# Weight tiles in another order, and a new plan of mixer steps, in a two-layer trunk on one core

## The chip, the core and the metric

The kernel runs on one core of a Trainium2 chip. A core has a matrix engine (PE in the profile; its weight loads are PEld), a vector engine (DVE), a scalar engine (ACT), a general engine (POOL) and a queue that issues transfers (SP). Each works through its own list of instructions in order, and they meet through semaphores. The metric is the device time of one launch in microseconds, the median of several runs. Less is better.

## What is computed

Two layers act on 256 tokens of width 1024, all in 32-bit floats. Cut to what matters:

```
a = rms_norm(h) ; proj = a @ w_in
da_q, da_k, da_v, z, xbc, dt, gla_q, gla_k, gla_v, gla_g, gla_lr = split(proj)
y_da  = differential attention: 4 heads, two softmaxes each, after a norm and a partial rotation of q and k
y_ssd = state-space mixer: conv of 4 taps and silu on xbc, two chunks of 128 tokens, gated by silu(z), norm
y_gla = linear attention: 4 chunks of 64, decays from gla_lr through log-sigmoid, norm, times silu(gla_g)
h = h + concat(y_da, y_ssd, y_gla) @ w_out
h = h + (silu(f @ w_gate) * (f @ w_up)) @ w_down          with f = rms_norm(h)
h = h + sigmoid(h @ ple_gate) * (p @ ple_proj)
```

## The kernel before, in words

All weights, some 133 MB, stream from memory once, in tiles of about 1 MB. Each tile is one unit of the list `units`. A unit's tile lands in a staging buffer `st` (three of them). ACT rounds it to a high part `wh` (L214) and DVE subtracts to get the low part `wl` (L215), both in halves of 1024 columns, with six halves of each kind in the pool. PE then makes three passes per block: high by high, high by low, low by high. The code loads two units ahead of the one that multiplies.

A layer has 19 units for the input products, 6 for the output product, 22 + 16 for the feed-forward part and 4 for the last gate. The change touches the first 25. Of the 19:

- `q0 q1 k0 k1 v0 v1 gv0 gv1 sg0 sg1` are halves of tiles with 512 columns (L884 to L886, 48 passes of 512 columns for a pair of halves). q, k, v belong to the attention, gv and sg are the value and the gate of the linear attention. A pair is read out of the accumulators at the end of its second half: q and k by four squares on ACT (L387) and four sums and products on DVE (L388, L389), v, gv and sg by two ACT instructions (L912).
- `x0` to `x3` (the four convolution tiles) and `gq`, `gk` have 256 columns (L263 to L265, 48 passes of 256 columns). A convolution tile leaves on DVE one product (L573) and six multiply-adds (L582), then a silu on ACT (L584).
- `z0`, `z1` (the state-space gate, the time steps `dt` and the input of the decays) and `ple` (the projection of p, L242 to L244).

Between the passes of a unit stand steps of the four mixers. They are Python generators: `gates` (3 steps), `ssd` (8), `gla` (5) and `da` (13). `PLAN` lists the units in their order, each with the steps that go into it, and `PLAN_OUT` does so for the output product. `spread` puts a unit's steps in a list, and at each `tick` (after 3 passes of an x-tile, 6 of the other kinds) one piece of a step is issued; `'-'` lets a tick go by:

```
        if pending:
            S, name = pending[0]
            with tc.issue_after(last.ins):
                done = name == '-' or step(S, name)
            if done:
                pending.pop(0)
```

Within this, the framework's scheduler decides at build time the order on each engine.

The steps that the prediction speaks of: the decays run L733, L740 (PE), L742 to L744 (ACT: absolute value, exponential, logarithm), L746 (DVE), L752 (PE), L755 and L756 (ACT exponentials). An attention block runs scores L484 and mask L491 (PE), maxima L499 and L500 (DVE), exponentials L504 (ACT, each with a sum that is read out), then L507, L508, L511, L512 (DVE), transposes L469 (PE), products with v L536, L540, L541 (PE). There are three blocks: one for the first 128 tokens and four heads, two for the second 128 tokens and two heads each. The linear attention ends with L817 and L826 (PE), the squares L395 (ACT), the norm L397, L184 to L194, L402 and the product with sg L837 (DVE), the transposes L845 (PE), and the two parts of `mix` L409 (ACT) and L410 (DVE), which the output product reads (L256, L258). PSUM has four banks for the accumulators `acc` and four for everything of the mixers, `pm`, which are used in turn: a mixer's matmul waits until the bank's last tile but three has been read.

Of the kernel before, what the change touches and what calls it, by code (L numbers as in the profile page):

```python
# [76 lines left out]
    ('x0', ()),  # L77
    ('x1', ()),
    ('x2', ()),
    ('z1', ()),  # L80
    ('gq', ()),
    ('x3', ('gates',)),
    ('k0', ('gates', 'ssd')),
    ('k1', ('-', '-', '-', '-', 'gates', 'ssd')),
    ('gk', ('da', 'da', 'ssd')),
    ('gv0', ('ssd',)),
    ('gv1', ('gla', '-', '-', 'da', 'da')),
    ('sg0', ('gla', 'ssd', 'gla')),
    ('sg1', ('-', 'da', 'ssd')),
    ('v0', ('ssd', '-', 'da', '-', 'da')),  # L90
    ('v1', ('ssd', 'da', '-', 'gla')),
    ('ple', ('da', '-', '-', 'da', '-', 'gla')),
]
PLAN_OUT = [('-', '-', 'da'), ('-', '-', 'da'), ('-', '-', 'da'), (), (), ()]


def _two_pi_parts():
# [11 lines left out]
def trunk_kernel(ctx: ExitStack, tc: tile.TileContext, a: dict):  # L109
# [752 lines left out]
    def spread(S, names, go, w):  # L862
        pending.extend((S, n) for n in names)
        go(w)
        while pending:
            tick(turn[0])
# [124 lines left out]
    def out_units(i, S, x):  # L991

        def first(c2):
            def go(w):
                for pb, c, _ in gemm_t(lambda c: (w, c * P), S["mix"][1] + S["mix"][2], True,
                                       0 if c2 else 4):
                    hv = h[:, 2 * c2 + c]
                    dve.tensor_tensor(hv, pb[:, :T], hv, ALU.add)
                    dve.tensor_tensor(hv, pb[:, T:], hv, ALU.add)
            return go  # L1000
# [13 lines left out]
        for c2 in range(4):  # L1014
            units.append((a["w_o1"][i, c2], KD, T,
                          lambda w, go=first(c2), c2=c2: spread(S, PLAN_OUT[c2], go, w)))
        for c4 in range(2):
# [228 lines left out]
```

## Time and profile before

| | |
|---|---|
| runs | 800.24, 800.93, 802.68 us; median 800.93 |
| the profiled execution | 800.33 us, span 798.1 us |
| PE busy | 778.2 us, 98% of the span |
| DVE, ACT busy | 640.9 us (80%), 477.4 us (60%) |
| granted clock of PE | 0.999 of full speed |

The busy share is a mean over the whole span. The 19 input units of the first layer end about 155 us after the span's start, and those of the second begin about 402 us and end about 548 us after it. The mixers' steps lie in these stretches.

### The profile page before, as it was taken

The page shows a single profiled execution, that of the slowest core. Times are in us where ns is not written, and L with a number is a line of the kernel's source. Part 1 is how long each engine was busy: PE and PEld are TensorE (multiplying, and loading weights), DVE is VectorE, ACT ScalarE, POOL GpSimd, SP SyncE. Part 2 cuts the span into 40 slices and gives each one's busy share as a digit, 9 for nine tenths or more (in the row PEclk, how much of TensorE's full clock was granted, in tenths as well). Part 3 has the DMA queues.
Part 4 walks back from the last instruction along what each step waited for, and adds up shares of the span by engine and source line. Part 5 has one row for each costly group of instructions (what it writes and reads, how often), then busy time and mean ns, then how long its engine had stood idle before and what let it go on. Part 6 is the DMA issues. An engine that isn't in the chain of part 4 may idle for free.

```text
span 798.1 us, 12793 instructions
## 1 busy us (share of the span) xinstructions
PE 778.2 (98%) x4810; PEld 682.7 (86%) x4810; DVE 640.9 (80%) x1341; ACT 477.4 (60%) x838; POOL 23.1 (3%) x36
## 2 busy tenths in 40 slices
PE   9999999899999999999999999997999999999997
PEld 6998877789888888888889988786998888888887
DVE  5998998888787777667799779988897777767674
ACT  7778537656665555555667585285466555554553
POOL 2000000002000000000020000000020000000000
PEclk9999999999999999999999999999999999999999
DMA  8763524244655543557555523433455555445641
GB/s 292 284 218 111 172 84 153 82 159 159 211 197 178 206 154 135 184 185 248 208 168 202 172 96 127 159 106 106 168 179 185 207 173 196 159 148 183 198 158 54
DMA packets 24302, 134.92 MB, mean 169 GB/s; under 512 B 2992, under 2 KB 5296, under 8 KB 11696
## 3 DMA queue, kind: packets, MB, share of 16 engines
q1 hardware_dynamic: 23904, 133.57, 48.8%
q8 instruction: 38, 0.62, 0.3%
q0 software_dynamic: 192, 0.52, 0.2%
q14 instruction: 24, 0.20, 0.1%
q10 hardware_dynamic: 144, 0.01, 0.0%
HBM read 133.05 MB, written 1.05 MB: 168 GB/s over the span
## 4 chain that ended last, share of the span: by engine, by line
PE 80%; DVE 14%; DMA 2%; ACT 2%; issue 1%; SPq 0%; DVEq 0%; ACTq 0%
PE acc L256 37%; PE acc L258 18%; DVE wl L215 4%; PE acc L265 4%; PE acc L264 4%; PE acc L263 4%; PE acc L884 2%; PE acc L886 2%; PE acc L885 2%; ACT e L504 1%; DMA h<-in_x 1%; PE acc L243 1%; PE acc L242 1%; PE acc L244 1%; DMA st<-in_w_z 1%
## 5 line engine op out<-in xcount | busy, mean ns | idle before, releaser
L214 ACT ACTIVATE wh<-st 128x1024 fp32r<-128x1024 f32 (+5 forms) x274 | 266.9, 979 | 231.0 <-PE acc L256 101.3
L215 DVE TENSOR_TENSOR wl<-st,wh 128x1024 fp32r<-128x1024 f32 (+5 forms) x274 | 308.5, 1128 | 100.3 <-ACT wh L214 99.8
L256 PE MATMUL acc<-x,wh 128*128 128x512 f32 x800 | 252.2, 396 | 0.1
L258 PEld LDWEIGHTS acc<-x,wl 128*128 128x128 f32 x800 | 150.3, 188 | 35.2
L258 PE MATMUL acc<-x,wl 128*128 128x256 f32 x800 | 157.2, 278 | 0.0
L256 PEld LDWEIGHTS acc<-x,wh 128*128 128x128 f32 x800 | 122.2, 189 | 1.4 <-DVE x L296 0.7
L256 PE MATMUL acc<-act,wh 128*128 128x512 f32 x352 | 111.9, 395 | 0.0
L258 PEld LDWEIGHTS acc<-act,wl 128*128 128x128 f32 x352 | 66.2, 188 | 14.3
L258 PE MATMUL acc<-act,wl 128*128 128x256 f32 x352 | 72.0, 279 | 0.0
L884 PE MATMUL acc<-wh,x 128*128 128x512 f32 x160 | 66.8, 420 | 0.5 <-DVE gate L301 0.4
L265 PE MATMUL acc<-x,wl 128*128 128x256 f32 x224 | 63.4, 283 | 0.9 <-DVE wl L215 0.9
L263 PE MATMUL acc<-x,wh 128*128 128x256 f32 x224 | 63.8, 285 | 0.0
L886 PE MATMUL acc<-wh,x 128*128 128x512 f32 x160 | 63.6, 397 | 0.0
L885 PE MATMUL acc<-wl,x 128*128 128x512 f32 x160 | 63.3, 396 | 0.2 <-DVE wl L215 0.2
L264 PE MATMUL acc<-x,wh 128*128 128x256 f32 x224 | 63.4, 283 | 0.0
L256 PEld LDWEIGHTS acc<-act,wh 128*128 128x128 f32 x352 | 54.9, 189 | 1.3
L265 PEld LDWEIGHTS acc<-x,wl 128*128 128x128 f32 x224 | 42.9, 192 | 1.1 <-DVE wl L215 1.1
L264 PEld LDWEIGHTS acc<-x,wh 128*128 128x128 f32 x224 | 42.9, 192 | 0.3
L263 PEld LDWEIGHTS acc<-x,wh 128*128 128x128 f32 x224 | 42.9, 191 | 0.3
L256 PE MATMUL acc<-mix,wh 128*128 128x512 f32 x128 | 40.8, 401 | 2.3 <-DVE mix L410 2.3
L301 DVE TENSOR_TENSOR gu<-acc,gu 128x256 f32<-128x256 f32 x88 | 36.8, 418 | 2.9 <-ACT gu L300 2.9
L884 PEld LDWEIGHTS acc<-wh,x 128*128 128x128 f32 x160 | 30.3, 190 | 6.9 <-ACT wh L214 0.7
(276 smaller groups left out, 1166.7 us busy)
## 6 DMA issues: line engine op xcount, KB each, us to landing
st<-in_w_f SPq DMA_DIRECT2D x44, 1024.0 KB, 4.9
st<-in_w_d SPq DMA_DIRECT2D x32, 704.0 KB, 4.1
st<-in_w_x SPq DMA_DIRECT2D x18, 1024.0 KB, 4.8
st<-in_w_o SPq DMA_DIRECT2D x12, 1024.0 KB, 5.0
st<-in_w_t SPq DMA_DIRECT2D x11, 1024.0 KB, 4.9
st<-in_w_g SPq DMA_DIRECT2D x8, 1024.0 KB, 4.9
st<-in_w_z SPq DMA_DIRECT2D x3, 1088.0 KB, 5.0
st<-in_w_x SPq DMA_DIRECT2D x8, 256.0 KB, 5.0
```

The lines of the kernel that those rows point to most:

```text
L214: i_hi = act.activation(wh[:, s], st[:, o], AF.Copy)
L215: i_lo = dve.tensor_tensor(wl[:, s], st[:, o], wh[:, s].bitcast(F32), ALU.subtract)
L242: pe.matmul(out, sh, mh, start=i == 0, stop=False)
L256: pe.matmul(out, wh[:, lo:lo + P], x[k], start=k == 0, stop=False)
L258: last = pe.matmul(out[:, :T], wl[:, lo:lo + P], x[k][:, :T], start=False, stop=k == n - 1)
L263: pe.matmul(out, sh, hi, start=k == 0, stop=False)
L264: pe.matmul(out, sh, x[k][:, T:], start=False, stop=False)
L265: last = pe.matmul(out[:, :T], sl, hi, start=False, stop=k == n - 1)
L301: dve.tensor_tensor(out, pb[:, :T], out, ALU.add)
L884: pe.matmul(pb[b], xh, wh, start=kk_ == 0, stop=False)
L885: pe.matmul(pb[b], xh, wl, start=False, stop=False)
L886: last = pe.matmul(pb[b], xl, wh, start=False, stop=kk_ == KD - 1)
```

## The change

The order of the units becomes: q0 q1 z0 x0 x1 x2 **x3 z1 sg0 sg1 k0 k1 gq gk** gv0 gv1 v0 v1 ple. Before it was: q0 q1 z0 x0 x1 x2 z1 gq x3 k0 k1 gk gv0 gv1 sg0 sg1 v0 v1 ple. So the last convolution tile comes ahead of z1, the gate sg comes from behind gv to a place ahead of k, and gq from ahead of x3 to behind k. The mixer steps are dealt anew over these units: the state-space steps stand in k0, k1, gq, gk, gv0, gv1, v0, v1 (before: k0, k1, gk, gv0, sg0, sg1, v0, v1), and one attention step less stands ahead of ple. The output product's plan differs in one entry. No instruction of the mixers or products is added or removed, and the tables hold for both layers.

```
     ('x2', ()),
+    ('x3', ()),
     ('z1', ()),
-    ('gq', ()),
-    ('x3', ('gates',)),
+    ('sg0', ()),
+    ('sg1', ('gates',)),
     ('k0', ('gates', 'ssd')),
...
-    ('v1', ('ssd', 'da', '-', 'gla')),
-    ('ple', ('da', '-', '-', 'da', '-', 'gla')),
+    ('v1', ('ssd', 'da', 'gla')),
+    ('ple', ('da', '-', '-', 'da', '-', 'gla', 'da')),
 ]
...
-PLAN_OUT = [('-', '-', 'da'), ('-', '-', 'da'), ('-', '-', 'da'), (), (), ()]
+PLAN_OUT = [('-', '-', 'da'), ('-', '-', '-', '-', 'da'), ('-', '-', 'da'), (), (), ()]
```

On ACT, in the first layer, this is where the decays (`ge`) are made, before:

```order
L742 ACTIVATE ge_885<-pm_882 128x512
L671 ACT_TABLE_LOAD
L671 ACTIVATE ce_897<-pm_894 128x16
L743 ACTIVATE ge_885<-ge_885 128x512
L214 ACTIVATE wh_1014<-st_1013 128x1024
L584 ACT_TABLE_LOAD
L584 ACTIVATE conv_857<-conv_857 128x512
L744 ACT_TABLE_LOAD
L744 ACTIVATE ge_885<-ge_885 128x512
```

and now:

```order
L742 ACTIVATE ge_898<-pm_895 128x512
L671 ACT_TABLE_LOAD
L671 ACTIVATE ce_910<-pm_907 128x16
L743 ACTIVATE ge_898<-ge_898 128x512
L214 ACTIVATE wh_1027<-st_1026 128x1024
L744 ACT_TABLE_LOAD
L744 ACTIVATE ge_898<-ge_898 128x512
```

The silu of the last convolution tile, with the table load for it, no longer stands between the exponential and the logarithm. The silu of sg moves ahead of L742. In all ACT has 17 table loads in its list instead of 23.

On DVE, the end of the third attention block and the start of the linear attention's norm (`fss`), before. sm_1586 and e_1590 belong to the second block, sm_1638 and e_1642 to the third, wl_1912 to a weight tile of the output product:

```order
L507 RECIPROCAL sm_1586<-sm_1586 128x2x2
L508 TENSOR_SCALAR sm_1586<-sm_1586,lam 128x2
L511 TENSOR_SCALAR e_1593<-e_1593,sm_1586 128x256 x2
L512 SCALAR_TENSOR_TENSOR e_1590<-e_1590,sm_1586,e_1593 128x256 x2
L507 RECIPROCAL sm_1638<-sm_1638 128x2x2
L508 TENSOR_SCALAR sm_1638<-sm_1638,lam 128x2
L410 SCALAR_TENSOR_TENSOR mix_1548<-pm_1667,par_70,mix_1548 128x128
L511 TENSOR_SCALAR e_1645<-e_1645,sm_1638 128x256 x2
L512 SCALAR_TENSOR_TENSOR e_1642<-e_1642,sm_1638,e_1645 128x256 x2
L215 TENSOR_TENSOR wl_1912<-st_1905,wh_1911 128x1024
L410 SCALAR_TENSOR_TENSOR mix_1549<-pm_1667,par_70,mix_1549 128x128
L397 TENSOR_REDUCE fss_1729<-fsq_1727 128x4
```

and now, with the third block's names sm_1673 and e_1677:

```order
L499 TENSOR_REDUCE mx_1672<-pm_1644 128x2
L410 SCALAR_TENSOR_TENSOR mix_1574<-pm_1627,par_70,mix_1574 128x128
L500 TENSOR_SCALAR mx_1672<-mx_1672 128x2x2
L410 SCALAR_TENSOR_TENSOR mix_1575<-pm_1627,par_70,mix_1575 128x128
L507 RECIPROCAL sm_1673<-sm_1673 128x2x2
L508 TENSOR_SCALAR sm_1673<-sm_1673,lam 128x2
L511 TENSOR_SCALAR e_1680<-e_1680,sm_1673 128x256 x2
L512 SCALAR_TENSOR_TENSOR e_1677<-e_1677,sm_1673,e_1680 128x256 x2
L397 TENSOR_REDUCE fss_1725<-fsq_1723 128x4
```

The second block has gone ahead, and between the third block's maxima (L500) and the use of its exponentials' sums (L507) only one short L410 is left.

On PE, from the second transposes of the linear attention's result (L845) on, before. acc_1868 is the last output of the ple projection, mix_1548 to mix_1551 the state-space result, acc_1915 an output of the output product:

```order
L845 MATMUL pm_1894<-cst,fyn_1755 128x128 x4
L256 MATMUL acc_1915<-mix_1548,wh_1781 128x512
L256 MATMUL acc_1915<-mix_1549,wh_1781 128x512
L258 MATMUL acc_1915<-mix_1548,wl_1782 128x256
L258 MATMUL acc_1915<-mix_1549,wl_1782 128x256
```

and now, with acc_1855 as the last output of ple:

```order
L845 MATMUL pm_1862<-cst,fyn_1751 128x128 x4
L242 MATMUL acc_1855<-ph_1038,wh_1615 128x256
L243 MATMUL acc_1855<-pl_1039,wh_1615 128x256
L244 MATMUL acc_1855<-ph_1038,wl_1616 128x256
L242 MATMUL acc_1855<-ph_1038,wh_1620 128x256
L243 MATMUL acc_1855<-pl_1039,wh_1620 128x256
L244 MATMUL acc_1855<-ph_1038,wl_1621 128x256
L536 MATMUL pm_1877<-v_1769,at_1670 128x128 x4
L256 MATMUL acc_1915<-mix_1572,wh_1774 128x512
L256 MATMUL acc_1915<-mix_1573,wh_1774 128x512
```

Six passes of ple and the attention's first products with v (L536) stood ahead of the transposes and stand behind them now.

## Rows read from the trace of the kernel before

**Rows 1.** The page: busy time, share of the span and instructions by engine.

```profile
PE 778.2 (98%) x4810; PEld 682.7 (86%) x4810; DVE 640.9 (80%) x1341; ACT 477.4 (60%) x838; POOL 23.1 (3%) x36
```

**Rows 2.** Waits of PE, whole span: waiter, releaser, total us, times, longest.

```profile
PE pm L845 <- DVE fyn L837: 4.1, 2, 2.0
PE pm L536 <- ACT v L912: 2.5, 2, 1.2
PE acc L256 <- DVE mix L410: 2.3, 2, 1.2
...
PE pm L484 <- DVE gst L804: 1.2, 2, 0.7
PE pm L484 <- ACT e L504: 1.1, 2, 0.6
```

**Rows 3.** DVE by windows, one in each layer: length, busy, clock, DMA, GB/s.

```profile
79.00:154.90 75.90, 70.73 (x198) 1.00 0.38 129
471.30:547.30 76.00, 70.74 (x198) 1.00 0.37 129
```

**Rows 4.** Longest wait of DVE between 79 and 155 us: total, times, longest.

```profile
DVE sm L507 <- ACT e L504: 2.5, 3, 1.7
```

**Rows 5.** Timeline of PE: start, length; passes of 512, of 256 columns, k's end.

```profile
134.64 0.39 PE L885 MATMUL acc<-wl,x 128*128 128x512 f32 x1
134.87 0.39 PE L886 MATMUL acc<-wh,x 128*128 128x512 f32 x1
...
182.90 0.28 PE L263 MATMUL acc<-mix,wh 128*128 128x256 f32 x1
183.02 0.28 PE L264 MATMUL acc<-mix,wh 128*128 128x256 f32 x1
...
77.02 0.28 PE L263 MATMUL acc<-x,wh 128*128 128x256 f32 x1
```

**Rows 6.** Timeline of DVE: the decays, k's eviction, a weight split, the last gate product.

```profile
72.95 0.69 DVE L746 SCALAR_TENSOR_TENSOR gk<-pm,ge 128x512 f32<-128x512 f32 x1 [2.67 <-ACT ge L744]
...
78.96 0.41 DVE L388 TENSOR_REDUCE dss<-dsq 128x4 f32<-128x256 f32 x1
...
81.58 1.22 DVE L215 TENSOR_TENSOR wl<-st,wh 128x1024 fp32r<-128x1024 f32 x1
82.72 0.37 DVE L426 TENSOR_SCALAR dv<-dss,rr 128x16 f32<-128x16 f32 x2
...
154.16 0.76 DVE L837 TENSOR_TENSOR fyn<-fyn,sg 128x256 f32<-128x256 f32 x2
```

**Rows 7.** Timeline of ACT around the decays.

```profile
69.05 1.28 ACT L584 ACT_TABLE_LOAD   x1
70.34 0.63 ACT L584 ACTIVATE conv<-conv 128x512 f32<-128x512 f32 x1
```

**Rows 8.** Timeline of DVE and of ACT: exponentials of the first and the third block.

```profile
123.97 0.17 DVE L500 TENSOR_SCALAR mx<-mx 128x8 f32<-128x8 f32 x1
127.18 0.20 DVE L507 RECIPROCAL sm<-sm 128x8 f32<-128x8 f32 x1 [1.73 <-ACT e L504]
...
140.51 0.47 ACT L504 ACTIVATE e<-pm,mx 128x256 f32<-128x256 f32 x1
142.21 0.22 ACT L504 ACTIVATION_READ_ACCUMULATOR e<-pm,mx 128x1 f32 x1
```

**Rows 9.** Timeline of PE from the linear attention's last products to the output product.

```profile
144.02 1.09 PE L826 MATMUL pm<-gst,gq 64*64 64x128 f32 x24
...
148.24 0.71 PE L536 MATMUL pm<-v,at 128*128 128x128 f32 x4 [1.22 <-ACT v L912]
...
154.73 0.79 PE L845 MATMUL pm<-cst,fyn 128*128 128x128 f32 x4 [2.03 <-DVE fyn L837]
155.27 0.72 PE L256 MATMUL acc<-mix,wh 128*128 128x512 f32 x2
...
161.26 1.20 PE L256 MATMUL acc<-mix,wh 128*128 128x512 f32 x4 [1.15 <-DVE mix L410]
```

More of the change, by code (lines that the diff above doesn't have):

```diff
@@ L79 @@
     ('x2', ()),
+    ('x3', ()),
     ('z1', ()),
-    ('gq', ()),
-    ('x3', ('gates',)),
+    ('sg0', ()),
+    ('sg1', ('gates',)),
     ('k0', ('gates', 'ssd')),
[L84 to L90, printed above, removed]
-    ('v1', ('ssd', 'da', '-', 'gla')),
-    ('ple', ('da', '-', '-', 'da', '-', 'gla')),
+    ('k1', ('-', '-', 'gates', 'ssd')),
+    ('gq', ('ssd', 'da', 'da')),
+    ('gk', ('ssd', '-', 'da')),
+    ('gv0', ('da', 'ssd')),
+    ('gv1', ('gla', 'ssd', '-', 'da')),
+    ('v0', ('gla', '-', 'da', 'ssd', 'gla')),
+    ('v1', ('ssd', 'da', 'gla')),
+    ('ple', ('da', '-', '-', 'da', '-', 'gla', 'da')),
 ]
-PLAN_OUT = [('-', '-', 'da'), ('-', '-', 'da'), ('-', '-', 'da'), (), (), ()]
+PLAN_OUT = [('-', '-', 'da'), ('-', '-', '-', '-', 'da'), ('-', '-', 'da'), (), (), ()]
 def _two_pi_parts():
```

## The prediction

> **What bounds the kernel now.** I read the page first. PE is busy for 778.2 of 798.1 us [rows 1], so 20 us is all that any reordering can return, and the start and the end of the program take part of it. The list of PE's waits says where the rest lies [rows 2]. The five largest belong to the input units and the step into the output product; together they make 11.2 us, half in each layer. Four are waits for DVE or ACT behind a mixer's step: the transposes of the linear attention's result wait for the gate product (L845, 4.1), the attention's first products for v (L536, 2.5), the output product for `mix` (L256, 2.3), the scores for a bank of PSUM (L484).
>
> The windows say why. From the eviction of k to the last gate product (L837), DVE works 70.73 of 75.90 us in the first layer and 70.74 of 76.00 in the second [rows 3]. In this stretch DVE is the bound and PE, with 3.2 us of waits at L536 and L845, follows it. The reader is to see in [rows 3] that the two layers behave alike, so I work out one and double it. The DVE idles 5.2 us in the stretch; 2.5 of that are three waits for the exponentials of an attention block [rows 4], the rest are smaller waits and the gaps between short dependent instructions.
>
> So the question for the new order is not how PE's work is laid, which stays the same, but when DVE enters this stretch, how much work lies in it, how long it idles there, and what PE still has to do when it ends.
>
> **The change part by part.** The sum is made against the profiled execution, 800.33 us with a span of 798.1; the median of the runs shown stands 0.6 above it.
>
> *Entry into the stretch.* Ahead of k's end PE gains the pair sg and loses gq. A pass of 512 columns follows its predecessor after 0.23 us, one of 256 columns after 0.12 [rows 5]; 48 passes each make 10.9 and 5.75, so k's products end 5.15 us later. Before, PE was through with k at 77.02 [rows 5] but DVE came to it at 78.96 [rows 6], 1.94 late. It was late because it had stood 2.67 us for the logarithm of the decays [rows 6], and the logarithm stood on ACT behind a table load and the silu of x3 [rows 7]. With x3 ahead this pair is gone from there. DVE then enters when the first square of k's eviction is read, some 0.4 after PE (an estimate from the 0.41 of L388's row, of the same size [rows 6]). Entry: +5.15 - 1.94 + 0.4 = +3.6. If the logarithm comes late all the same, +5.15; less than +3.6 only if PE were faster, for which there is no reason.
>
> *Work in the stretch.* The same mixer instructions stand in it, and gq's eviction comes in. But one unit less is multiplied behind k, and by the order of the DVE list three weight splits (L215) have left the stretch. A split holds DVE for 1.14 us, from 81.58 to the next instruction at 82.72 [rows 6]; gq's product is of 512 columns like L746 (0.69 [rows 6]), some 0.6 of it by itself. So -3 x 1.14 + 0.6 = -2.8. This is a count and has little play: -2.2 to -3.0.
>
> *Idle time in the stretch.* Of the 5.2 before, 2.7 are not exponentials, and I keep 2.4 of them. The first block's eight exponentials run from 124.1 to 127.2, and DVE stood 1.73 at their end [rows 8]; now the masked copies of the linear attention and a norm of the state-space mixer stand in between, and I leave 0.5. Four exponentials of a later block last from 140.51 to 142.43 [rows 8], 2.1 with the start. Behind the second block's maxima DVE has one split of 1.14, which leaves 0.95. Behind the third block's it has one short L410, taken as 0.25 (its 128 columns are half of the 256 that L388 takes 0.41 for [rows 6]), which leaves 1.85; before, the second block's end and a split lay there. Last, the second block's scores need a bank that the first block's exponentials read, which is the kind of wait that L484 shows [rows 2]: 0.6. Sum: 2.4 + 0.5 + 0.95 + 1.85 + 0.6 = 6.3, or +1.1. The bounds are 2.4 (every exponential covered) and 10 (each block waited for in full, 3.1 + 2.1 + 2.1, and the 2.4). I take 6.3, since the third block's wait has nothing in the order that could cover it.
>
> *From the last gate product on.* Before, from the start of the second L845 at 154.73 to the first product that needs the linear attention's `mix` at 161.26, 6.53 us passed, with a wait of 1.15 at the end [rows 9]. Now PE has there the transposes (0.54, up to 155.27 [rows 9]), six passes of ple (6 x 0.12), four products of L536 (0.5) and the same 4.85 of state-space products and L540, L541 (161.26 - 1.15 - 155.27, rounded up), 6.6 with nothing waited for. The parts of `mix` have all this time to land, where before they took it with a head norm and three splits ahead of them on DVE. Result: 0, between -0.3 and +0.5. So L536's and L256's waits go, but what lay ahead of L845 as cover has gone behind it. The wait at L845 grows: from the end of L826 at 145.1 to the end of L837 at 154.9 [rows 6, 9] DVE needs 9.8 in any order, and PE now has 12 passes of ple, then L845, then 6 passes, and two sets of transposes ahead of them: 18 x 0.12 + 3 x 0.54 = 3.8. That leaves some 6 per layer at L845 and at the transposes of the third block just before it.
>
> *Covered edits.* Six table loads go; but for the pair at the logarithm, already counted, they lie on ACT, which is busy for 60% [rows 1] and idles before weight conversions. Four convolution tiles in a row give DVE no more work than PE has beside it, since the weight splits run two units ahead; if this cover failed, the first product of z1 would wait, at most for one split. The tiles' transfers are the same in number and size, and SP and POOL get no other work. The later attention step in the output product has a second unit's time to land.
>
> Sum for a layer: 3.6 - 2.8 + 1.1 + 0 = +1.9; I take 1.7 to 1.9, and for two layers +3.5. From 800.33 this gives 803.8, and with half of the 0.6 to the median 804.1.
>
> A rule speaks otherwise. A table load shows 1.28 us, and the silu starts right behind it, at 70.34 after 69.05 + 1.28 [rows 7]. The Trainium skill (ScalarE: Activation LUTs, What ACT_TABLE_LOAD costs) asks for another 1.38 us of drain at each switch, 2.66 in all, and its Table sets section tells to batch calls by set, which this change does. By that page six switches would be worth 16 us, to about 785; by the row they are worth 7.7 of ACT's time. The trace shows no drain ahead of this load, so the row decides.
>
> **The rivals.**
>
> *Faster: DVE's waits are covered.* If the scheduler's list has enough between L500 and L507 after all, because ACT, with three loads less per layer, comes earlier, the idle time falls to 2.4, and a layer makes 3.6 - 2.8 - 2.8 = -2.0. That is 796.3 by the profiled execution, 796.8 by the median. For it: the 1.73 at the first block is the longest wait of DVE here and does go [rows 4, 8]. Against it: the third block.
>
> *No change.* If idle time stays at about 4.5 instead of 6.3, entry and work cancel: 801. For it: the same DVE work bounds the same stretch, and only its entry has moved.
>
> *Slower by more.* The logarithm is late all the same, and all blocks' exponentials are waited for: entry +5.15, idle +3.5, 5.9 a layer, 812; half of it is 807.
>
> *The loads are on the path.* Each of the six that go is then worth its row, 1.28 [rows 7], 7.7 in all: 793. For it only the 2.67 at the logarithm [rows 6], which the sum holds already.
>
> **How the numbers follow.** What can be told from no change here is 0.3%, or 2.4 us: 798.5 to 803.3 counts as the same. My forecast has a chance of 0.45, with a range of its own of 801.5 to 807; of it 0.27 lies over 803.3 and 0.18 under. The faster rival has 0.25, nearly all of it under 798.5 (0.23). No change has 0.18. Slower by more has 0.09, and the loads on the path 0.03. Faster: 0.23 + 0.03 = 0.26. Slower: 0.27 + 0.09 = 0.36. Same: 0.38. The range goes from 796.3, the faster rival's centre, to 808, past half of the slower rival; it leaves out half of the faster one's lower side, the loads and the rest of the slower one, about 0.2.
>
> **What would show it.** The eviction of k (L388) should begin at about 82.6 in the first layer and the last L837 at 156 to 157, with DVE busy for about 68 in between. The logarithm's wait at L746 should be shorter than 2.67. PE's waits at L536 and at L256 for `mix` should be gone, those at L845 and L469 should make about 12 for both layers, and DVE should wait close to 1.8 at the L507 of the third block. The prediction is wrong in its root if DVE is not busy for nine tenths of this stretch, in its entry if L388 begins much before 82, and in its idle time if the waits at L507 come to less than 2 us a layer.

## The result, and the profile after

The changed kernel takes 811.64 us (median of 4 runs, 811.30 to 812.46), the kernel before 800.61 (median of 4, 800.24 to 802.68): the ratio estimated from the single executions is 1.0123, 95% interval [1.0105, 1.0141], in which the quotient of the two medians, 1.0138, lies. It is slower, by 11 us, where 3 were forecast. The profiled execution took 812.46 us, with a span of 810.3.

The program has one landmark in each half layer, the products of the token norm (L316). Timeline of PE, before and then after (start, length, instruction):

```profile
24.11 0.50 PE L316 MATMUL pm<-ones,ssq 128*128 128x1 f32 x4
199.22 0.50 PE L316 MATMUL pm<-ones,ssq 128*128 128x1 f32 x4
413.13 0.50 PE L316 MATMUL pm<-ones,ssq 128*128 128x1 f32 x4
591.67 0.50 PE L316 MATMUL pm<-ones,ssq 128*128 128x1 f32 x4
```

```profile
24.79 0.50 PE L316 MATMUL pm<-ones,ssq 128*128 128x1 f32 x4
205.38 0.51 PE L316 MATMUL pm<-ones,ssq 128*128 128x1 f32 x4
419.28 0.50 PE L316 MATMUL pm<-ones,ssq 128*128 128x1 f32 x4
603.87 0.50 PE L316 MATMUL pm<-ones,ssq 128*128 128x1 f32 x4
```

From the first to the second lie the mixers and the output product: 175.1 us before, 180.6 after. From the second to the third lies the feed-forward part, 213.9 in both. So of the 12.2 us of span 0.7 is the start, 5.5 the first layer's mixers and, in the same way, 6.0 the second layer's.

The page after, busy time by engine, answers to [rows 1]: the same 4810 instructions of PE, and six fewer of ACT, the table loads.

```profile
PE 786.7 (97%) x4810; PEld 687.1 (85%) x4810; DVE 642.9 (79%) x1341; ACT 470.8 (58%) x832; POOL 23.2 (3%) x36
```

DVE's stretch from k's eviction to the last gate product, the row ahead of it, its first and its last row in the timeline, and the windows of both layers (length; busy time and instructions of PE, PEld, DVE, ACT, POOL; granted clock; DMA share; GB/s), against [rows 3, 6]:

```profile
82.70 0.68 DVE L602 TENSOR_TENSOR xd<-pm,par 128x512 f32<-128x512 f32 x1
83.30 0.41 DVE L388 TENSOR_REDUCE dss<-dsq 128x4 f32<-128x256 f32 x1
...
158.33 0.76 DVE L837 TENSOR_TENSOR fyn<-fyn,sg 128x256 f32<-128x256 f32 x2
```

```profile
83.30:159.10 75.80, 68.15 (x448) 55.55 (x447) 68.61 (x196) 37.30 (x88) 0.00 (x0) 0.98 0.31 113
480.90:556.80 75.90, 68.83 (x452) 56.13 (x450) 68.59 (x196) 37.45 (x88) 0.00 (x0) 0.99 0.32 113
```

The stretch begins 4.3 us later by the clock and is as long as before, with 2.1 us less work of DVE and 2.0 more idle time. That the work is less holds for the stretch alone. From the layer's first L316 to the end of the last L837, DVE (length; busy time and instructions; clock; DMA) has the same 321 and 303 instructions and nearly the same work, before and then after:

```profile
24.11:154.92 130.81, 120.11 (x321) 1.00 0.45 156
413.13:547.32 134.19, 118.27 (x303) 1.00 0.42 145
```

```profile
24.79:159.09 134.30, 120.43 (x321) 0.99 0.43 152
419.28:556.81 137.53, 119.04 (x303) 1.00 0.41 142
```

Three weight splits have gone from behind the eviction to ahead of it. Of the 3.5 and 3.3 us by which this longer stretch grows, 3.2 and 2.6 are idle time of DVE. The waits of DVE from the eviction on (first layer), against [rows 4], and of PE over the whole span, against [rows 2]:

```profile
DVE wl L215 <- ACT wh L214: 2.2, 2, 1.2
DVE sm L507 <- ACT e L504: 2.1, 2, 1.5
```

```profile
PE pm L845 <- DVE rs_v L184: 4.3, 2, 2.2
PE pm L845 <- DVE fyn L837: 4.0, 2, 2.1
PE pm L779 <- DVE yf L194: 2.7, 2, 1.6
...
PE pm L817 <- ACT at L471: 1.4, 2, 0.7
```

The waits at L536 and at L256 for `mix` are gone, as forecast; those at L845 have doubled. What the forecast did not hold stands in the clock column of three windows around the second L845 (first layer; the second has the same at 555.7 to 562.5) and in PE's timeline:

```profile
149.50:156.30 6.80, 4.07 (x31) 3.30 (x30) 5.91 (x25) 4.41 (x9) 0.00 (x0) 1.00 0.00 0
156.30:163.10 6.80, 4.91 (x23) 4.55 (x23) 5.09 (x15) 3.40 (x8) 0.00 (x0) 0.50 0.00 0
163.10:169.90 6.80, 6.80 (x46) 6.16 (x46) 4.91 (x14) 2.57 (x3) 0.00 (x0) 1.00 0.45 149
```

```profile
155.18 0.86 PE L845 MATMUL pm<-cst,fyn 128*128 128x128 f32 x4 [2.17 <-DVE rs_v L184]
...
158.90 1.15 PE L845 MATMUL pm<-cst,fyn 128*128 128x128 f32 x4 [1.89 <-DVE fyn L837]
...
160.06 0.41 PE L243 MATMUL acc<-pl,wh 128*128 128x256 f32 x1
160.27 0.41 PE L244 MATMUL acc<-ph,wl 128*128 128x256 f32 x1
```

For 6.8 us TensorE is granted half its clock, the lower of its two levels, 1.2 instead of 2.4 GHz. A pass of 256 columns follows the one ahead of it after 0.21 us there, where [rows 5] shows 0.12. Ahead of the fall PE had worked 4.07 of 6.80 us and stood for 2.17 us at the first L845; the wait of 1.89 us at the second lies behind the fall. The profile of before has the full clock at this place in both layers.

### The profile page after: what moved, and what is told of

The parts are those of the page before. It is cut to its first block, busy times and chain, and to the rows that moved or that the text cites. A ratio compares the mean times of both kernels' runs of the same rounds, so it can differ in the third digit from the quotient of the medians.

```text
span 810.3 us, 12785 instructions
## 1 busy us (share of the span) xinstructions
PE 786.7 (97%) x4810; PEld 687.1 (85%) x4810; DVE 642.9 (79%) x1341; ACT 470.8 (58%) x832; POOL 23.2 (3%) x36
## 4 chain that ended last, share of the span: by engine, by line
PE 77%; DVE 15%; ACT 3%; DMA 2%; issue 2%; SPq 0%; ACTq 0%; DVEq 0%; POOL 0%; POOLq 0%
PE acc L256 37%; PE acc L258 18%; DVE wl L215 5%; PE acc L265 3%; PE acc L263 3%; PE acc L264 3%; PE acc L884 2%; PE acc L886 2%; PE acc L885 2%; DMA h<-in_x 1%; ACT wh L214 1%; DVE conv L582 1%; PE acc L243 1%; PE acc L244 1%; PE acc L242 1%
## 5 line engine op out<-in xcount | busy, mean ns | idle before, releaser
L215 DVE TENSOR_TENSOR wl<-st,wh 128x1024 fp32r<-128x1024 f32 (+5 forms) x274 | 308.6, 1129 | 115.5 <-ACT wh L214 115.0
L214 ACT ACTIVATE wh<-st 128x1024 fp32r<-128x1024 f32 (+5 forms) x274 | 267.4, 979 | 217.7 <-PE acc L256 101.8
L256 PE MATMUL acc<-x,wh 128*128 128x512 f32 x800 | 252.3, 396 | 0.1
L256 PEld LDWEIGHTS acc<-x,wh 128*128 128x128 f32 x800 | 122.2, 189 | 1.4 <-DVE x L296 0.7
L256 PE MATMUL acc<-act,wh 128*128 128x512 f32 x352 | 111.8, 395 | 0.0
L256 PEld LDWEIGHTS acc<-act,wh 128*128 128x128 f32 x352 | 54.9, 189 | 1.3
L256 PE MATMUL acc<-mix,wh 128*128 128x512 f32 x128 | 41.8, 409 | 0.0
```

Source lines behind the costliest of these rows:

```text
L214: i_hi = act.activation(wh[:, s], st[:, o], AF.Copy)
L215: i_lo = dve.tensor_tensor(wl[:, s], st[:, o], wh[:, s].bitcast(F32), ALU.subtract)
L256: pe.matmul(out, wh[:, lo:lo + P], x[k], start=k == 0, stop=False)
```

## The experiments

Theory A, formed on these rows: two things make the loss. TensorE's queue reaches the output product later because it waits more, and the waits at L845 bring a half clock that costs by itself. Theory B is the prediction's account: the end of the stretch is its entry plus DVE's work plus idle time. All results but e5's are medians with the ratio to the kernel before measured beside it. The table gives the times in the traces (us after the layer's own first L316, layer 1 / layer 2), worked out from timeline rows as shown above; the columns give starts, of the last instruction where "last" is said; "to norm" is from the start of the last L837 to the second L316, "half" the time at half clock from one L316 to the other.

| kernel | k's eviction | last L826 | last L837 | second L316 | to norm | half |
|---|---|---|---|---|---|---|
| before | 54.9 / 58.1 | 120.7 / 124.1 | 130.4 / 133.8 | 175.1 / 178.5 | 44.7 / 44.8 | 0 / 0 |
| after | 58.5 / 61.6 | 124.7 / 127.9 | 133.9 / 137.1 | 180.6 / 184.6 | 46.7 / 47.5 | 6.8 / 6.8 |
| e1 | 58.5 / 61.6 | 124.8 / 127.9 | 133.9 / 137.1 | 179.7 / 182.9 | 45.8 / 45.8 | 0 / 0 |
| e13 | 58.4 / 61.6 | 124.6 / 127.9 | 133.8 / 137.1 | 178.6 / 181.9 | 44.8 / 44.8 | 0 / 0 |
| e2 | 59.0 / 61.6 | 124.3 / 128.7 | 133.5 / 138.0 | 178.7 / 182.8 | 45.2 / 44.8 | 6.8 / 10.2 |
| e3 | 54.8 / 58.1 | 121.2 / 124.6 | 130.5 / 133.9 | 177.2 / 181.3 | 46.7 / 47.4 | 6.8 / 6.8 |
| e4 | 58.6 / 61.6 | 136.5 / 137.7 | 146.1 / 147.3 | 192.3 / 194.5 | 46.2 / 47.3 | 23.9 / 20.5 |
| e5 | 54.8 / 58.1 | 120.7 / 126.1 | 130.4 / 135.8 | 175.1 / 181.0 | 44.7 / 45.2 | 0 / 10.2 |
| e6 | 54.8 / 58.1 | 120.7 / 126.0 | 130.3 / 135.7 | 176.1 / 181.5 | 45.7 / 45.8 | 0 / 6.8 |
| e7 | 58.5 / 61.6 | 124.7 / 127.9 | 131.5 / 134.7 | 177.0 / 181.6 | 45.5 / 46.9 | 0 / 3.4 |
| e8 | 54.8 / 58.1 | 120.7 / 124.1 | 128.2 / 131.5 | 173.0 / 176.3 | 44.8 / 44.8 | 0 / 0 |
| e9 | 58.7 / 61.6 | 121.4 / 124.4 | 131.5 / 134.5 | 181.7 / 185.0 | 50.2 / 50.5 | 10.2 / 10.2 |
| e10 | 59.0 / 62.8 | 123.9 / 124.8 | 133.6 / 134.2 | 180.9 / 180.6 | 47.3 / 46.4 | 6.8 / 6.8 |
| e11 | 43.7 / 47.1 | 123.1 / 127.1 | 132.6 / 136.6 | 178.8 / 184.1 | 46.2 / 47.5 | 6.8 / 6.8 |
| e12 | 55.7 / 59.5 | 118.3 / 122.2 | 126.6 / 130.5 | 171.2 / 175.2 | 44.6 / 44.7 | 0 / 0 |
| e14 | 52.2 / 53.3 | 118.7 / 121.7 | 127.2 / 130.0 | 171.9 / 174.7 | 44.6 / 44.6 | 0 / 0 |

### The half clock

**e1**, passes that keep PE at work ahead of L845 (the changed kernel):

```diff
             pt = bank()
+            for n in range(8):
+                pe.matmul(v3(pt, 4), idb, negb.unsqueeze(1).to_broadcast([P, 4, P]), start=True, stop=True)
             for n in range(4):
                 pe.transpose(pt[:, n * P:(n + 1) * P], ys[e][:, n * P:(n + 1) * P], ident)
```

> The changed kernel, with eight extra passes of 512 columns (no result is kept of them, the transposes overwrite it) ahead of each of the two sets of transposes at L845, where TensorE waits 2.17 and 1.89 us. The order of the other instructions up to the last gate product is the same. Theory (the half clock after these waits is a cost of its own, set off by TensorE standing idle there): the granted clock stays full in both layers, the last gate product stays at about 158.7 us, and from it to the first product of the feed-forward part some 2 us less pass, 46.7 to about 44.7; two layers make 4 to 5, so 811.6 becomes about 807. Rival (the clock's fall is incidental, the rest of the loss lies in the order): 811 to 812, whether the clock falls or not. Rival (the passes come in the way): 8 x 0.23 = 1.8 us ahead of each set, some of it on the path: 812 to 814.

809.28 us, 1.0077 [1.0056, 1.0098]. The clock stays full and the last L837 is where it was; the gain is half of what was expected. The passes had to wait for their bank, which L402 frees, and so ended 1.2 us after the gate product was there. **e13** has three of them (`range(3)`), which end in time:

> The changed kernel with three instead of eight extra passes ahead of each set of transposes at L845. The eight ended 1.2 us after the gate product was there, since their bank came free only with L402; three (0.69) end before it. Theory (the half clock is worth what lies between 46.7 and 47.5 us of the changed kernel behind its last L837 and the 44.7 of before): if the clock stays full, 44.7 to 45.0 in both layers, and 811.6 - 2.1 - 2.9 = 806.6; if three passes don't keep it, no change from 811 to 812. Rival (the extra passes themselves gave the gain, or the clock is worth less): the clock full, but 809 or more.

807.60 us, 1.0082 [1.0051, 1.0114]. The window ahead and the one that was at half clock, and the second set of transposes (two lines further down in this kernel's source):

```profile
149.50:156.30 6.80, 4.89 (x33) 3.63 (x32) 5.80 (x27) 4.28 (x9) 0.00 (x0) 1.00 0.00 0
156.30:163.10 6.80, 5.25 (x37) 4.53 (x37) 5.19 (x13) 4.08 (x8) 0.00 (x0) 1.00 0.01 2
```

```profile
157.85 0.81 PE L845 MATMUL pm<-negb,idb 128*128 128x512 bf16 x3 [1.58 <-DVE fyn L402]
...
158.49 0.70 PE L847 MATMUL pm<-cst,fyn 128*128 128x128 f32 x4
```

With everything ahead of L845 at its old place (table), "to norm" falls from 46.7 and 47.5 to 44.8 and 44.8, that of the kernel before. The half clock costs 1.9 and 2.7 us, 4.5 of the 12.2. This is shown, since nothing ahead of it moved.

**e5** is the kernel before, unchanged. Its 48 executions beside the experiments spread from 799.7 to 804.6: the four with a mean granted clock of 0.999 took 799.7 to 800.8, the seven with 0.990 took 803.5 to 804.6. The trace read for the prediction, with 0.999, is thus of a rare kind.

> The kernel before, unchanged, with a trace of its own. Its executions on this chip spread from 799.7 at a mean granted clock of 0.999 to 804.6 at 0.990, where the executions shown ahead of the prediction had 0.999. Theory (the half clock is a cost of its own): this trace has one or two stretches of half clock if its time is over 801, behind TensorE's waits at L536 and L845, and everything up to them stands where it stood (last gate product 130.4 us after the first L316); each stretch costs some 2 us behind it. Rival (the clock is incidental): the time differs, but the rows up to the output product differ with it, or the stretch of half clock costs nothing.

803.12 us, clock 0.992. Layer 1 agrees with the first trace to 0.1 us. Layer 2 has two stretches of half clock, one of them here:

```profile
502.00:508.80 6.80, 6.12 (x36) 4.57 (x35) 6.75 (x13) 1.75 (x3) 0.00 (x0) 1.00 0.45 154
508.80:515.70 6.90, 6.90 (x29) 5.13 (x28) 6.74 (x14) 1.06 (x1) 0.00 (x0) 0.51 0.71 211
```

It makes the last L837 2.0 us late, the other, behind it, 0.4. So the kernel before loses 2.4 us to the clock in this execution, and nothing in the one that I read. The slower executions have the lower clocks, but those with 0.994 lie anywhere from 800.3 to 804.1, so a mean clock alone does not give the time. Here PE had one wait of 0.7 us (L484) in the window ahead of the fall and worked 6.12 of its 6.80 us; in e13 it worked 4.89 us in the window of the first row above and kept the clock. What tips it in one execution and not in another stays open. The Trainium skill (TensorE: Matmul & The Clock Gate, What's actually happening) says that the clock gate follows how busy TensorE has been and that half is its state after idleness. The rows agree in direction (in the trace of the changed kernel each fall stands behind a wait of some 2 us at L845, and e13, with passes in place of part of it, has none; the other three executions, clock 0.992 to 0.993, have no trace), but no single wait ahead of a fall was longer than 2.2 us.

**e6**, e1's edit in the kernel before:

> The kernel before with the same eight extra passes (their result is overwritten) ahead of each set of transposes at L845. Theory (half clock as its own cost): the clock stays near 1.0 in every execution, so the spread from 799.7 to 804.6 shrinks to about 1 us, at 800 to 801.5, with up to 1 us lost where the passes outlast the wait. Rival (the spread has another source): the same median and the same spread as the kernel before. Rival (the passes are in the way): 2 to 3 us slower than 802.8.

804.33 us, 1.0027 [1.0012, 1.0042]: not faster. In its trace "to norm" is 1.0 longer in both layers (passes in the way) and the half clock behind L484's waits is still there in the second layer: the passes cover only their own place.

### The tiles' order and the attention's late step, apart

**e2**, the new order with the end of the old plan:

```diff
-    ('gv0', ('da', 'ssd')),
+    ('gv0', ('da', 'ssd', 'da')),
-    ('v1', ('ssd', 'da', 'gla')),
-    ('ple', ('da', '-', '-', 'da', '-', 'gla', 'da')),
+    ('v1', ('ssd', 'da', '-', 'gla')),
+    ('ple', ('da', '-', '-', 'da', '-', 'gla')),
-PLAN_OUT = [('-', '-', 'da'), ('-', '-', '-', '-', 'da'), ('-', '-', 'da'), (), (), ()]
+PLAN_OUT = [('-', '-', 'da'), ('-', '-', 'da'), ('-', '-', 'da'), (), (), ()]
```

> The new order of the weight tiles, but the attention's steps one earlier, so that the end of the plan (v1, the embedding tile, the output product) is that of the kernel before. Theory of two parts: k's eviction at about 83.3 as in the changed kernel (entry +3.6), less DVE work in the stretch (-2.1), idle time near the 5.2 of before or one above, and with the attention's L536 again ahead of L845 no half clock: 2 x (3.6 - 2.1 + 0.5) = +4 on the kernel before, about 805. Rival (the order of tiles carries the whole loss): 811 to 812. Rival (the late attention step carries it): 800 to 801.

**e3**, the old order with the late step (in the kernel before):

```diff
-    ('gv1', ('gla', '-', '-', 'da', 'da')),
+    ('gv1', ('gla', '-', '-', 'da')),
-    ('v1', ('ssd', 'da', '-', 'gla')),
-    ('ple', ('da', '-', '-', 'da', '-', 'gla')),
+    ('v1', ('ssd', 'da', 'gla')),
+    ('ple', ('da', '-', '-', 'da', '-', 'gla', 'da')),
-PLAN_OUT = [('-', '-', 'da'), ('-', '-', 'da'), ('-', '-', 'da'), (), (), ()]
+PLAN_OUT = [('-', '-', 'da'), ('-', '-', '-', '-', 'da'), ('-', '-', 'da'), (), (), ()]
```

> The order of the weight tiles of before, with the attention one step later from gv1 on and the end of the plan (v1, the embedding tile, the output product) of the changed kernel. Theory of two parts: entry unchanged (k's eviction at 79.0), the last gate product within 1 us of 154.5, but the cover ahead of L845 gone, so longer waits there and a half clock behind it: 2 x (2 to 3) on the kernel before, 804.5 to 807. Rival (the order of tiles carries the whole loss): 800 to 801. Rival (the late step carries it): 811 to 812.

e2: 806.53 us, 1.0044 [1.0031, 1.0057]. e3: 804.71, 1.0025 [1.0010, 1.0040]. By the table e3 leaves the last L837 where it was (0.1 later) and has the whole half clock, 2.0 and 2.6 us; e2 has the L837 3.2 and 4.2 later and 0.4 and 0.1 behind it. So the new order, with its steps dealt anew, makes the stretch end late, and the late step brings the half clock behind it. That it does so by taking L536 away from ahead of L845 is argued, from e13's cover at that place. Since e2's stretch holds half clock of its own, its 3.2 and 4.2 are not the order's alone.

### What sets the end of the stretch

**e11**, k ahead of sg in the changed kernel, with the steps at their places in the row of units:

```diff
-    ('sg0', ()),
-    ('sg1', ('gates',)),
-    ('k0', ('gates', 'ssd')),
-    ('k1', ('-', '-', 'gates', 'ssd')),
+    ('k0', ()),
+    ('k1', ('gates',)),
+    ('sg0', ('gates', 'ssd')),
+    ('sg1', ('-', '-', 'gates', 'ssd')),
```

> The changed kernel with the pair k ahead of the pair sg; the steps stay at the same places in the row of units. Theory B, the account of the prediction (end = entry + work + idle): k's eviction 10.9 us earlier, four splits (4.6) more behind it, so the last L837 some 6 us earlier in each layer: 799 to 800. Theory A (the place of the mixers' steps in the row of units and TensorE's queue set the end): the eviction is earlier by the same, VectorE idles or does other work, and the last L837 stays within 1 us of 158.7: 810 to 812.

809.66 us, 1.0099 [1.0080, 1.0117]. k's eviction is 14.8 us earlier, the last L837 1.3 and 0.5. DVE's longer stretch (68.0 to 156.8) has 10.4 us of idle time, and the waits have grown (the second row is DVE alone, from the layer's first L316):

```profile
68.00:156.80 88.80, 83.27 (x528) 67.86 (x527) 78.45 (x207) 52.14 (x106) 0.00 (x0) 0.98 0.34 120
24.18:157.23 133.05, 120.93 (x321) 0.99 0.43 154
```

```profile
DVE sm L507 <- ACT e L504: 4.8, 3, 2.1
DVE mix L410 <- ACT mix L409: 2.0, 1, 2.0
```

Theory B falls here. The stretch is 13.0 us longer than in the changed kernel (88.80 against 75.80): 9.8 of that is more work of DVE (78.45 against 68.61) and 3.2 more idle time. The work is not new. Three splits and steps of the state-space mixer and the decays that stood ahead of k's eviction now stand behind it, and from the layer's first L316 on DVE works 120.9 us, where the changed kernel works 120.4. The terms of the prediction's sum are a correct ledger of a stretch, but not causes: moving the eviction moves work from one side of it to the other.

**e9**, the linear attention's products ahead of the attention's third block:

```diff
-    ('v1', ('ssd', 'da', 'gla')),
+    ('v1', ('ssd', 'gla', 'da')),
```

> The changed kernel with the last two steps at v1 in the other order: the linear attention's products (L817, L826) ahead of the attention's transposes and its third block's scores. In the changed kernel TensorE's queue has L469 ahead of them, which waits for a bank and then for ACT, so the last L826 ends at 149.68 instead of 145.1. Theory A (this place in the queue makes the stretch longer than the sum of VectorE's work): the last L826 ends at about 146, the last L837 comes some 3 us earlier in each layer, 805 to 806. Theory B (VectorE's work and its idle time of 7.2 bound the stretch wherever these products stand): the last L837 within 1 us of 158.7, 810 to 812. Rival (the attention is late in their place): L837 earlier, but the output product's second half waits: 811 or more.

812.68 us, 1.0134 [1.0112, 1.0156]. The last L826 is 3.3 and 3.5 us earlier, the last L837 2.4 and 2.6, and then all is lost:

```profile
PE pm L469 <- DVE fyn L402: 8.4, 2, 4.2
```

The attention's transposes now stand behind and wait 4.2 us a layer for a bank of PSUM that the head norm holds. PE's queue does set the place of L837, but moving a step in it only moves the wait.

**e10**, eight buffers instead of six for the upper part of the weights, against DVE's waits of 2.2 for the conversion L214:

```diff
-NSLOT = 49
+NSLOT = 45
-            wh = wp.tile([P, WSLOT // 2], F32R, tag="whi", bufs=NHALF, name=nm("wh"))
+            wh = wp.tile([P, WSLOT // 2], F32R, tag="whi", bufs=8, name=nm("wh"))
```

> The changed kernel with eight instead of six buffers for the converted weights' upper part (and 45 instead of 49 general slots, to make room). In the changed kernel VectorE waits 2.2 us a layer for such a conversion (L215 for L214), and ACT stands 2.23 and 1.26 us just before them for a buffer that TensorE still reads. Theory (this wait is the part of the idle time that the prediction lacked): the wait falls under 0.5, the last L837 comes 1 to 2 us earlier in each layer, 807.5 to 809.5. Rival (the wait is a consequence of TensorE being late, and goes elsewhere): 811 to 812. Rival (four slots less make new waits): 812 or more.

808.09 us, 1.0082 [1.0060, 1.0104]. The wait is gone in both layers. In layer 2 the last L837 comes 2.9 us earlier; in layer 1 only 0.3, because the exponentials are waited for instead:

```profile
DVE sm L507 <- ACT e L504: 4.1, 2, 2.1
```

In one layer it was a real loss, in the other it went elsewhere. The same edit makes the feed-forward part between the layers 1.0 us shorter (212.9 us from the second L316 to the third), so not all of its gain lies in the mixers.

**e4**, five splits a layer on GpSimd:

```diff
-                i_lo = dve.tensor_tensor(wl[:, s], st[:, o], wh[:, s].bitcast(F32), ALU.subtract)
+                i_lo = (pool if len(split_at) % 67 in range(14, 19) and k0 else dve).tensor_tensor(wl[:, s], st[:, o], wh[:, s].bitcast(F32), ALU.subtract)
```

> The changed kernel, with five weight splits per layer (the second half of the tiles gv0, gv1, v0, v1 and the embedding's) on GpSimd instead of VectorE. Theory (VectorE is the bound of the stretch): at 1.14 us a split the last gate product comes 4 to 5 us earlier in each layer, near 154, until the next bound: 811.6 - 2 x 4 to 5 = 802 to 804, and less by up to 2 x 2 where the shorter waits at L845 keep the clock: 798. Rival (the stretch waits for ACT and the chains of short steps, not for VectorE's work): 810 to 812. Rival (GpSimd is slow at it or hinders VectorE, and the products wait for the split): 813 or more. No split of this kind on GpSimd is in the traces so far.

833.28 us, 1.0374 [1.0351, 1.0397]. A group of such splits on GpSimd (busy, mean ns), and one on DVE that ran beside another:

```profile
L215 POOL TENSOR_TENSOR wl<-st,wh 128x1024 fp32r<-128x1024 f32 x10 | 26.0, 2602 | 130.4 <-ACT wh L214 98.1 <-DVE dss L388 28.2 <-DVE dt__181_1090 L192 4.1
```

```profile
84.98 3.26 DVE L215 TENSOR_TENSOR wl<-st,wh 128x1024 fp32r<-128x1024 f32 x1
```

A split takes 2.6 us there, and DVE's own, begun 0.2 us behind one at 84.76, takes 3.26 where 1.22 is usual [rows 6]. Two others on DVE, begun ahead of GpSimd's, kept their 1.21 and 1.22 us, and there GpSimd's took 3.26 and 3.21 instead of some 2.4. A step of a norm's chain on two columns, of some 0.16 us otherwise, took 2.34 beside another split:

```profile
494.17 1.21 DVE L215 TENSOR_TENSOR wl<-st,wh 128x1024 fp32r<-128x1024 f32 x1
494.38 3.26 POOL L215 TENSOR_TENSOR wl<-st,wh 128x1024 fp32r<-128x1024 f32 x1 [36.08 <-ACT wh L214]
...
129.19 2.34 DVE L192 TENSOR_TENSOR rs_t<-yf 128x2 f32<-128x2 f32 x1
```

The times fit the one that began later standing until the other had ended: the split at 84.76 ended at 87.16, and from there to DVE's end at 88.24 is 1.1 us. The Trainium skill (GPSIMD Engine Reference, 1. Specifications) says that GpSimd shares its SBUF interfaces with VectorE, with contention for instructions of two SBUF inputs; these rows agree. The test therefore says nothing of whether less work on DVE would help.

### Less work on DVE, and a faster kernel

**e7**, the linear attention's two head norms as one chain on eight columns (the changed kernel; lines behind it are nine further), and **e8**, the same in the kernel before:

```diff
+        for e in range(2):
+            sq = slot("fsq")
+            act.activation(sq, po[e], AF.Square)
+            dve.tensor_reduce(ssm[:, 4 * e:4 * e + 4], v3(sq, 4), AX.X, ALU.add)
+        with soon():
+            dve.tensor_scalar(vm, ssm, 1.0 / P, EPS, op0=ALU.mult, op1=ALU.add)
+            rsqrt_of(fm, vm, tm)
         for e in range(2):
-            yn = head_norm(po[e])
+            yn = slot("fyn")
+            dve.tensor_tensor(v3(yn, 4), v3(po[e], 4), headed(fm[:, 4 * e:4 * e + 4], 4, P), ALU.mult)
```

> The changed kernel, with the two head norms of the linear attention (one chain of twelve short dependent steps of some 0.2 us each per half) done as one chain on eight columns: TensorE's and ACT's instructions are the same in the same order, VectorE has twelve short steps less per layer. Theory (VectorE's chain behind the last L826 decides when the stretch ends): the last L837 comes about 2.4 us earlier in each layer (158.7 to 156.3) and the waits at L845 shrink by as much: 811.6 - 4.8 = 806.8 with the half clock still there, 802 to 803 if the shorter waits keep the clock up. Rival (the output product is held by something else behind it, such as the weights or the attention's tail): L837 earlier, but 810 to 812.

> The kernel before with the same merged head norms. Theory: the same chain ends its stretch, so about 2 us a layer, 798 to 799 where the kernel before makes 802.8 on this chip, and below 798 if the clock stays up. Rival (TensorE with its 98% is the bound and the chain is hidden): 802 to 803.

e7: 805.68 us, 1.0047 [1.0032, 1.0063]. e8: 796.27, 0.9924 [0.9904, 0.9944], with a clock of 1.000. The last L837 comes 2.4 us earlier in every layer of e7 and 2.2 in e8: behind the last L826 the chain of short steps is the path in both kernels. It is therefore no part of the difference between them.

**e12**, the convolution tiles together in e8's kernel, the lists of steps at their places:

```diff
-    ('z1', ()),
-    ('gq', ()),
-    ('x3', ('gates',)),
+    ('x3', ()),
+    ('z1', ()),
+    ('gq', ('gates',)),
```

> The kernel before with the merged head norms (796.3), and with x3 moved ahead of z1 and gq, the steps at their places: the part of the change that batches the convolution tiles' silu and takes table loads out from ahead of the decays. Theory B (entry counts in full): k's eviction 1.5 to 1.9 us earlier per layer and the time 793. Theory A (the steps' places set the end): k's eviction earlier, the last L837 within 0.5 us, 796 to 797. Rival (every table load on the path, 1.28 each): 4 to 6 loads less, 789 to 791.

**e14**, besides this k ahead of gq:

```diff
-    ('gq', ('gates',)),
-    ('k0', ('gates', 'ssd')),
-    ('k1', ('-', '-', '-', '-', 'gates', 'ssd')),
+    ('k0', ('gates',)),
+    ('k1', ('gates', 'ssd')),
+    ('gq', ('-', '-', '-', '-', 'gates', 'ssd')),
```

> The kernel of 793.7 us (before, merged head norms, x3 early) with the pair k ahead of gq. k's eviction comes 5.75 us earlier. Account of the prediction (entry counts): 2 x 3 or more faster, under 788. Theory A (the place of the steps in the row of units sets the end): 793 to 794.5.

e12: 793.69 us, 0.9898 [0.9881, 0.9916]. e14: 793.56, 0.9902 [0.9877, 0.9926], the same. The time of e12 is the one theory B gave, the way is not: k's eviction comes 0.8 and 1.4 us later than in e8, and the last L837 still 1.6 and 1.0 earlier. From the eviction on DVE has 65.50 us of work where e8 had 69.01, since three splits and a product now stand ahead of it, and PE works almost without a gap (first layer, e8 and then e12; the second row of each is DVE from the layer's first L316 to the last L837):

```profile
79.30:153.10 73.80, 70.56 (x446) 57.97 (x446) 69.01 (x186) 41.72 (x92) 0.00 (x0) 1.00 0.39 132
24.45:153.04 128.59, 118.27 (x309) 1.00 0.45 158
```

```profile
80.10:151.50 71.40, 71.14 (x439) 56.44 (x439) 65.50 (x182) 41.61 (x92) 0.00 (x0) 1.00 0.35 122
24.46:151.48 127.02, 118.50 (x309) 1.00 0.45 160
```

From that first L316 to the last L837 DVE idles 8.5 us in e12 and 10.3 in e8, so here too the end follows the idle time and not the work. Of the table loads only one in all has gone, 22 against 23, where 4 to 6 were expected. And e14's eviction is 3.4 and 6.2 us earlier than e12's for nothing. That agrees with e11.

With e7, e12 gives the parts of the stretch. Both have the merged norms and the convolution tiles together; they differ in the place of sg and gq (with the steps laid for it) and in the late step, which by e3 is worth 0.1 there. The last L837 is 4.9 and 4.2 us later in e7. The convolution tiles together are worth -1.6 and -1.0 (e12 against e8). The sums, 3.3 and 3.2, are by their making e7 against e8, the change's cost with merged norms; without them it is 3.5 and 3.4.

## Why the prediction was wrong

*Entry, +3.6.* The eviction came 3.7 and 3.5 us later (58.5 against 54.9, 61.6 against 58.1), and DVE's wait at L746 fell from 2.67 to 0.72. The number is right, in part by luck: the eviction was to wait for its first square, but it begins at the end of L602 at 83.30, with no wait, and stood behind the same step before. As a step towards the end it is wrong: e11 and e14 move the same eviction by 3 to 15 us and the end by at most 1.3. And what L746 gave back was lost ahead of the eviction: DVE's waits for conversions there (L215 for L214) grew from 1.1 to 4.1 us in the first layer and from 6.7 to 9.1 in the second.

*Work, -2.8.* Measured 68.61 against 70.73, so -2.1. The count of three splits was right, but they only went to the other side of the eviction: counted from the layer's start, DVE's work is 0.3 and 0.8 us more. So the later entry and the smaller work are in large part the same splits, counted once on each side, and what moved the end is DVE's idle time.

*Idle time, +1.1.* Measured +2.0. The attention's blocks were seen rightly in kind: no wait at the first, 0.6 and 1.5 at the others (0.5, 0.95 and 1.85 forecast). What was missing is the 2.2 for the conversions on ACT, which themselves wait for a weight buffer that PE still reads; I had put such waits under "smaller waits" and kept them as they were. By e10 they were worth 0.3 us in one layer and 2.9 in the other.

*From the last gate product on, 0.* This step failed. At full clock it holds: e13 has 44.8 against 44.7, with L536 and the passes of ple behind L845 as counted. But the measured time is 2.0 and 2.7 longer, by the half clock. I had worked out that some 6 us a layer of waits would crowd at L845 and L469 (it was 4.1 and 0.3), took them as hidden behind DVE's chain, and went on with 0.12 us a pass behind them; the rows show 0.21. The trace that I read has the full clock at this place throughout, and no rival of mine had another one.

*The sum.* Per layer: +1.9 forecast for the stretch, +3.5 and +3.4 measured; 0 forecast behind it, +2.0 and +2.7 measured; and 0.7 at the start, for which no cause was sought. The list of PE's five largest waits leaves out one of 1.5 us at the program's start (L167), which is larger than both at L484; nothing in the sum rests on it. The rival "slower by more" has the right time, 812, and a wrong mechanism: the logarithm was not late, and the first block's exponentials were covered. The faster rival and "no change" needed 2.4 and 4.5 us of idle time in the stretch; it was 7.2. "The loads are on the path" is not borne out: six went and the kernel got slower, and e12, with one load less, is faster than e8 by 2.6 us in the medians.

*What stays open.* The place of sg and gq, with the steps laid for it, costs 4 to 5 us a layer if the late step is worth as little there as in e3, but which of the waits in between is the cause is not settled. The trace shows that the linear attention's last state (L807), before and after, comes some 22 us later in the layer:

```profile
121.83 0.49 DVE L807 TENSOR_SCALAR gst<-gst,ex 128x128 f32<-128x128 f32 x2
```

```profile
144.53 0.47 DVE L807 TENSOR_SCALAR gst<-gst,ex 128x128 f32<-128x128 f32 x2
```

Its products, DVE's backlog (L779 waits 1.6 for a bank) and the attention's transposes (L817 waits 0.7 for L471) then meet in the last four units; e9 and e10 each took one of these away, and it came back in another wait in one or both layers. An order that keeps the new place of sg and has no such wait wasn't tried.

## What to carry to other kernels

When an engine's waits are gathered in one place, price not only the waits but the clock behind them, and look at more than one execution before you take the clock as given: three passes without a result ahead of the waiting instruction were worth 4 us here (e13), and eight that ended too late half of it (e1). A stretch's entry, work and idle time add up, but a mark that moves past the engine's own work changes entry and work together; count the work from a mark that stays, here the layer's first product. Moving the eviction did not push the end, and shortening a chain of short dependent steps at the end (2.4 us) did. Split a change before judging it: its convolution tiles together with merged norms give 793.7 us, better than both kernels, while the rest of it, the late step and its half clock with it, costs 12 (e7 against e12).

## What the runs showed of the hardware

The half clock comes and goes between executions of one and the same program: the kernel before took 799.7 us at a mean clock of 0.999 and 804.6 at 0.990, with four of 48 executions at 0.999, while e12, in which PE hardly waits, stayed at 0.999 to 1.000 and within 793.5 to 793.8. And a two-input subtraction on GpSimd stretched the same on VectorE, begun just behind it, from 1.22 to 3.26 us, and a step on two columns from 0.16 to 2.34; where VectorE's began first, GpSimd's took 3.26 instead of some 2.4 (e4).
